# Experts: tokens sorted by expert group, so that a pair of experts works on two or three of four token tiles

## The chip, the cores and the metric

One core of one Trainium2 chip runs the whole program. The metric is device microseconds of one execution, as the median of the runs shown; lower is better. Engines are named as the profile names them: PE is TensorE's matmuls, PEld its weight loads, DVE VectorE, ACT ScalarE, POOL GpSimd, SP SyncE, which here only issues transfers.

## The reference

A decoder layer on 512 tokens of 1024 numbers, in float32: a mixer of four branches, cross attention into 256 memory tokens, and a mixture of experts. After each of the three, `x = layer_norm(alpha * x + y)`. The change touches the third part and the last layer norm:

```python
def hier_moe(x, rg_w, rg_b, re_w, re_b, w_gu, w_down):       # 512 tokens, 4 groups of 8 experts
    p_grp = softmax(xt @ rg_w + rg_b)                        # 4 groups
    grp = argmax(p_grp)                                      # one group for each token
    p_e = softmax((xt @ re_w + re_b)[rows, grp])             # 8 experts of that group
    top_p, top_i = top_k(p_e, 2)                             # two of them
    w = p_grp[rows, grp] * top_p / sum(top_p)
    expert_idx = grp * 8 + top_i
    # for each token: sum over its two experts of
    #   w * ((silu(x @ gate) * (x @ up)) @ down)             gate, up: 1024 x 512 each, down: 512 x 1024
```

## The kernel before

The tokens lie in four tiles of 128 rows, `xt[0]` to `xt[3]`, 1024 numbers each. After the cross attention, `spread(q)` (line 1196) normalises a tile in place and splits it into a high and a low part, `XH[q]` and `XL[q]`, since a float32 value goes through TensorE's one-pass form as two such parts. Routing follows tile by tile: `route` finds group and experts, `place` counts the rank of each token within its expert, and `sid` becomes 64 x expert + rank: every expert has 64 slots (`SLOT`), and no expert has more tokens than that in these inputs. `overflow` (line 1732), inside a runtime `If`, would serve the rest.

The expert stage, `moe` (line 1787), takes the 32 experts in 16 pairs p = 0 to 15, 128 slots a pair, and two pairs share one gather. For each pair, in this order on TensorE:
- `hidden`, eight steps k: the slots' inputs `xg` times gate and up weights, float32, two experts in the two halves of the array; each step uses two chunks of 512 KB. Then silu and product on ACT and DVE (`activate`), and four transposes (`turn`);
- `combine` of the pair before: for each token tile and half row two one-pass products with the one-hot matrix `ohT` (which slot feeds which token) add the weighted outputs `yh` and `yl` to `xt`, eight such groups;
- after odd pairs `gather` (with `collect` and `deliver`): for four column blocks and four token tiles, products of `XH` and `XL` with the one-hot matrices `oh` collect the tokens of the next 256 slots; ACT scales them by the second layer norm's gains and writes `xg`;
- `down`, four quarters of two chunks each, then `scaled` writes `yh` and `yl`.

In the first two pairs there is more: `route_weights` and `token_rows` (line 1389: the slot numbers and weights laid along rows, needed by `slot_rows`), `rejoin` (POOL adds `XH` and `XL` back into `xt`), `gains` and `regain` (the second layer norm's gain and bias on `xt`). The last two pairs run through `finish` (line 1599), written out by hand: `down` quarters, `spill` (their share of combine), `add`, `square`, and the third layer norm with the output, by halves of tiles; two halves (`SHARED`) are done on ACT and POOL.

Order: TensorE, VectorE and ScalarE keep the order of the code from line 1034 on, and SyncE's queue likewise in `moe`. The weights come through that queue, 24 chunks a pair, 384 in all, into a ring of 29 places (`chunk`, `eat`): a chunk is requested when the one 29 before it has been used up (`eat`). Seven further chunks of the first pair have places of their own (`once`), four of them in `xt`. So 36 chunks are there before the stage begins.

## Time and profile before

| | us |
|---|---|
| median of three runs | 1118.59 (1116.53 to 1119.81) |
| the profiled execution | 1120.17 |
| its span | 1118.5 |

| share of the span | PE | PEld | DVE | ACT | POOL |
|---|---|---|---|---|---|
| busy | 96% | 66% | 51% | 37% | 12% |

The page divides the span into 40 slices and shows busy shares in tenths; TensorE is at 9 in almost all, the DMA at 9 from slice 26 to 38, where it moves 408 to 409 GB/s. All times within the span are counted from its start. The expert stage begins near 618 us. A matmul in float32 is two records of the profile; records of the two halves of the array overlap, and matmul ends are modelled, so a busy PE is not PE at its peak.

### The profile page before, as it was taken

The numbers are of one execution on the slowest core, as the hardware profiler recorded it, in microseconds if no ns is written. First come the engines' busy times: TensorE is split into PE (matmuls) and PEld (weight loads), VectorE is DVE, ScalarE is ACT, GpSimd is POOL, SyncE is SP. The second block draws the span as 40 slices with busy tenths as digits, with TensorE's granted clock in tenths as the row PEclk, the third lists the DMA queues.
The fourth block names the chain that finished last, engine by engine and source line by source line (L and its number), as shares of the span: only waits on it lengthen the run. The fifth ranks groups of instructions, "written<-read, shape, count | busy, mean of one in ns | idle before, by whom it ended". The sixth has DMA issues, their size and how long they took to land. (4 is left out here: it accounts for less than half of the span.)

```text
span 1118.5 us, 15296 instructions
## 1 busy us (share of the span) xinstructions
PE 1073.0 (96%) x5818; PEld 741.9 (66%) x5818; DVE 571.4 (51%) x1214; ACT 408.5 (37%) x767; POOL 131.6 (12%) x131
## 2 busy tenths in 40 slices
PE   7999999999999999998998999999989999999993
PEld 6688777777888777787867555564655464656452
DVE  6436656878855633654558163524260433334426
ACT  6326647567544423433445312121203021212023
POOL 1000002302211112334124030000000000000003
PEclk9999999999999999998999899999999999999997
DMA  6612222112222213765363778999999999999982
GB/s 241 235 57 76 76 76 95 57 57 95 96 84 76 76 58 101 299 216 174 130 261 110 305 296 342 409 409 408 409 408 408 409 408 409 409 409 409 409 350 75
DMA packets 75052, 263.49 MB, mean 236 GB/s; under 512 B 8416, under 2 KB 8704, under 8 KB 74976
## 3 DMA queue, kind: packets, MB, share of 16 engines
q1 hardware_dynamic: 73440, 257.81, 60.2%
q0 software_dynamic: 1248, 4.15, 1.1%
q8 instruction: 47, 0.77, 0.3%
q10 hardware_dynamic: 288, 0.52, 0.1%
q14 instruction: 29, 0.24, 0.1%
HBM read 260.36 MB, written 2.10 MB: 235 GB/s over the span
## 5 line engine op out<-in xcount | busy, mean ns | idle before, releaser
L236 PE MATMUL acc<-ring,xg 128*64 128x512 f32 x724 | 167.6, 592 | 0.0
L228 DVE TENSOR_TENSOR wl<-raw,wh 128x1024 fp32r<-128x1024 f32 x63 | 78.5, 1247 | 88.9 <-PE mm L236 41.6
L236 PEld LDWEIGHTS acc<-ring,xg 128*64 128x64 f32 x724 | 54.3, 137 | 98.3 <-issue 94.0
L236 PE MATMUL mm<-XH,wh 128*128 128x512 f32 x392 | 106.1, 400 | 5.9 <-ACT XH L220 5.2
L227 ACT ACTIVATE wh<-raw 128x1024 fp32r<-128x1024 f32 x71 | 75.0, 1057 | 97.0 <-PE mm L236 59.0
L236 PE MATMUL mm<-XL,wh 128*128 128x512 f32 x392 | 106.7, 398 | 0.0
L236 PE MATMUL mm<-XH,wl 128*128 128x512 f32 x392 | 106.2, 397 | 0.0
L236 PEld LDWEIGHTS mm<-XH,wh 128*128 128x128 f32 x392 | 73.2, 190 | 23.7 <-ACT XH L220 5.2
L1596 DVE SCALAR_TENSOR_TENSOR yl<-t,ws,yh 128x512 fp32r<-128x512 f32 x28 | 20.8, 750 | 127.7 <-ACT yh L1595 127.7
L236 PEld LDWEIGHTS mm<-XH,wl 128*128 128x128 f32 x392 | 73.4, 189 | 18.8 <-issue 3.8
L236 PEld LDWEIGHTS mm<-XL,wh 128*128 128x128 f32 x392 | 73.0, 189 | 16.0 <-issue 1.2
L236 PE MATMUL t<-ring,hh 128*64 128x256 f32 x696 | 81.8, 381 | 0.0
L1557 ACT ACTIVATE hh<-acc 128x512 f32<-128x512 f32 x15 | 9.0, 597 | 173.2 <-PE acc L236 162.7
L1558 DVE TENSOR_TENSOR hh<-hh,acc 128x512 f32<-128x512 f32 x15 | 10.3, 688 | 117.7 <-PE acc L236 106.5
L236 PEld LDWEIGHTS t<-ring,hh 128*64 128x64 f32 x696 | 51.0, 137 | 27.0 <-issue 2.1
L1465 ACT ACTIVATE xg<-acc,gbt 128x128 f32<-128x128 f32 x128 | 47.9, 461 | 44.0 <-PE acc L236 44.0
L852 POOL TENSOR_TENSOR mix<-mix,gate 128x512 f32<-128x512 f32 x24 | 37.7, 1573 | 191.2 <-DVE gate L851 173.5
L1710 POOL TENSOR_TENSOR stat<-stat,mhalf 128x2 f32<-128x2 f32 x2 | 2.3, 1154 | 447.9 <-DVE stat L1709 447.9
L1595 ACT ACTIVATE yh<-t,ws 128x512 fp32r<-128x512 f32 x28 | 19.0, 688 | 82.2 <-PE t L236 69.2
L236 PE MATMUL s<-in,in 128*128 128x256 f32 (+5 forms) x198 | 43.8, 342 | 0.7 <-ACT S L626 0.7
L1497 DVE SCALAR_TENSOR_TENSOR xt<-xt,s 128x512 f32<-128x512 f32 x60 | 38.4, 681 | 7.9 <-PE s L236 7.9
L555 ACT ACTIVATE S<-S,sm 128x128 f32<-128x128 f32 (+3 forms) x48 | 26.6, 555 | 38.4 <-DVE sm L553 38.1
(449 smaller groups left out, 2011.1 us busy)
## 6 DMA issues: line engine op xcount, KB each, us to landing
ring<-gu SPq DMA_DIRECT2D x193, 512.0 KB, 10.2
ring<-dn SPq DMA_DIRECT2D x93, 512.0 KB, 10.2
XL<-gu SPq DMA_DIRECT2D x36, 512.0 KB, 10.2
raw<-wing SPq DMA_DIRECT2D x32, 512.0 KB, 3.3
raw<-gu SPq DMA_DIRECT2D x26, 512.0 KB, 10.2
XL<-dn SPq DMA_DIRECT2D x16, 512.0 KB, 10.2
raw<-winf SPq DMA_DIRECT2D x15, 512.0 KB, 3.2
raw<-dn SPq DMA_DIRECT2D x13, 512.0 KB, 10.2
```

What stands on the lines that cost most here:

```text
L227: self.nc.scalar.activation(h, r, AF.Copy)
L228: (self.nc.gpsimd if pool else self.nc.vector).tensor_tensor(l, r, f32(h), op=ALU.subtract)
L236: self.nc.tensor.matmul(out, lhsT, rhs, start=start, stop=stop, skip_group_check=True)
L555: nc.scalar.activation(s[:, :n], s[:, :n], AF.Exp, bias=sm[:, 0, q:q + 1], scale=-1.0, accum_out=sm[:, 1, q:q + 1])
L852: nc.gpsimd.tensor_tensor(mix[d], mix[d], g, op=ALU.add)
L1465: self.nc.scalar.activation(t[:, d, :], p[:, d - 2 * b, w * k:w * k + w], AF.Identity, scale=self.gbt[:, d:d + 1], bias=self.gbt[:, NK + d ...
L1497: self.nc.vector.scalar_tensor_tensor(z, z, scale, p, op0=ALU.mult, op1=ALU.add)
L1557: self.nc.scalar.activation(h, pg[0], AF.Silu)
L1558: self.nc.vector.tensor_tensor(h, h, pg[1], op=ALU.mult)
L1595: nc.scalar.activation(yh[:, cs], py[ch], AF.Copy, scale=ws)
L1596: nc.vector.scalar_tensor_tensor(yl[:, cs], py[ch], ws, f32(yh[:, cs]), op0=ALU.mult, op1=ALU.subtract)
L1710: nc.gpsimd.tensor_tensor(w(11), w(5), self.mhalf.to_broadcast([128, 2]), op=ALU.pow)
```

## The change

- In the routing stage, `records` puts what belongs to a token (experts, ranks, weights, its number, its group) into one tile `rec`; `sort` works out each token's place in an order sorted by group, and the routing weights are worked out there as well. `spread` also writes each normalised tile to memory (`zd`), by ACT's queue.
- In pair 0, `sort_records` moves the records into sorted order by products with the permutation, and `use_records` makes the index lists and marks tokens that lie outside the tiles that their group may use (`SPAN`); any such token sends the program into the overflow loop. `token_rows` now comes after `down`.
- `rejoin` fetches the rows of `zd` into `xt` by index, a transfer by POOL for each tile, instead of adding `XH` and `XL`. `respread` splits the sorted tiles again: tiles 0 and 1 in pair 1, ahead of its activation, tiles 2 and 3 in pair 2 with POOL.
- `gains` uses two other banks and gains scaled by alpha; `regain` runs on tiles 0 and 1 in pair 1 and on tiles 2 and 3 at the end of pair 2. Pair 1's order is now gains, turn, regain, gather, gains, regain, combine, down.
- `onehots`, `gather`, `slot_rows`, `combine` and `spill` run over the tiles of the group's span: two for the first and last four pairs, three for the others.
- Token tiles 0 and 1 are normalised and written out in pairs 9 and 13 (`settle`), tiles 2 and 3 at the end. All output goes through POOL by index (`ship`), at the end in halves of tiles. The gains of the third layer norm are loaded in pair 8 by POOL.

```diff
-SHARED = ((0, 0), (0, 1))
+SPAN = (0, 1), (0, 1, 2), (1, 2, 3), (2, 3)
...
     def gains(self, ps, ch):
...
-            p = self.t(ps, [128, 512], F32, "acc", 4)
+            p = self.t(ps, [128, 512], F32, "s", 2)
...
     def rejoin(self):
         self.xt = [self.t(self.right, [128, 1024], F32, f"xt{q}", 1) for q in range(NT)]
-        for cs in (slice(0, 512), slice(512, 1024)):
-            for q in range(NT):
-                self.nc.gpsimd.tensor_tensor(self.xt[q][:, cs], f32(self.XH[q][:, cs]), f32(self.XL[q][:, cs]), op=ALU.add)
-
-    def regain(self, ch, gb):
         for q in range(NT):
+            self.nc.gpsimd.indirect_dma_start(out=self.xt[q], out_offset=None, in_=self.zd[:, :],
+                                              in_offset=bass.IndirectOffsetOnAxis(ap=self.idx[:, q:q + 1], axis=0))
+
+    def respread(self, qs, low):
+        for q in qs:
+            self.nc.scalar.activation(self.XH[q], self.xt[q], AF.Copy)
+            low.tensor_tensor(self.XL[q], self.xt[q], f32(self.XH[q]), op=ALU.subtract)
...
             def spread(q):
                 z = self.xt[q]
                 nc.scalar.activation(z, z, AF.Identity, scale=stat[q][:, 5:6], bias=stat[q][:, 6:7])
+                nc.scalar.dma_start(self.zd[128 * q:128 * q + 128, :], z)
                 nc.scalar.activation(self.XH[q], z, AF.Copy)
...
             self.collect(hot[3], 3, range(4))
+            self.sort(mq, ps)
...
+    def sort(self, mp, ps):
...
+        p = self.t(ps, [128, 512], F32, "s", 2)
+        self.mm(p[:, 0:E], ones, self.cum[NT - 1], True, True)
+        self.mm(p[:, 64:80], ones, flat(run), True, False)
+        self.mm(p[:, 64:80], self.tri[:, 0:128], flat(grp), False, True)
+        nc.vector.tensor_tensor(flat(pr), p[:, 64:80], flat(grp), op=ALU.mult)
+        nc.vector.tensor_reduce(pos[:, 0], pr.rearrange("p g q -> p q g"), axis=AX.X, op=ALU.add)
+        nc.vector.tensor_scalar(pos[:, 1], pos[:, 0], -256.0, None, op0=ALU.add)
+        self.route_weights(mp, p)
+        self.pos = pos
+
+    def permutation(self, mp):
...
+            for i in range(2):
+                self.nc.vector.tensor_scalar(t[:, 256 * i:256 * i + 256], self.mc[:, _M_IOTA:_M_IOTA + 256], self.pos[:, i, q:q + 1], None, op0=ALU.is_equal)
+            self.perm.append(t)
+
+    def sort_records(self, ps):
+        p = self.t(ps, [128, 512], F32, "s", 2)
+        for t in range(NT):
+            for q in range(NT):
+                self.mm(p[:, 8 * t:8 * t + 8], self.perm[q][:, 128 * t:128 * t + 128], self.rec[:, q], q == 0, q == NT - 1)
+        return p
...
     def slot_rows(self, mp, p):
         nc = self.nc
+        span = SPAN[p // 4]
+        cs = slice(128 * span[0], 128 * span[-1] + 128)
...
     def gather(self, ps, oh, dst, work=iter(())):
         for b in range(4):
             p = self.t(ps, [128, 2, 256], F32, "acc", 4)
-            for q in range(NT):
-                self.collect(oh[q], q, [b], {b: p})
+            for q in oh:
+                self.collect(oh[q], q, [b], {b: p}, min(oh), max(oh))
...
-    def combine(self, ps, rows, ohT, yh, yl, scale=1.0, wide=False):
-        for i in range(2 * NT):
-            ch, q = divmod(i, NT)
+    def combine(self, ps, rows, ohT, yh, yl, tiles=range(NT), wide=False, sums={}):
+        for i in range(2 * len(tiles)):
+            ch, q = i // len(tiles), tiles[i % len(tiles)]
...
+    def ship(self, q, h=None):
+        if h is None:
+            ix, o, z = self.idx[:, q:q + 1], self.a["out"], self.xt[q]
+        else:
+            ix, o, z = self.idx2[:, q, h:h + 1], self.a["out"].rearrange("t (h c) -> (t h) c", h=2), self.xt[q][:, 512 * h:512 * h + 512]
+        self.nc.gpsimd.indirect_dma_start(out=o, out_offset=bass.IndirectOffsetOnAxis(ap=ix, axis=0), in_=z, in_offset=None)
+
+    def settle(self, q, stat):
+        for ch in range(2):
+            self.norm_square(stat, q, ch, self.t(self.m0, [128, 512], F32, "wt", 2))
+        self.norm_stats(stat)
+        self.norm_rstd(stat)
+        self.norm_apply(self.xt[q], stat, self.gb3)
+        self.ship(q)
...
         def spill(b, j):
-            for q in range(NT):
-                if j == 0 and q % 2 == 0:
+            for n, q in enumerate(span):
+                if j == 0 and n == 0:
...
         def apply(q, h):
-            z, _, b, o = part(q, h)
-            nc.vector.scalar_tensor_tensor(z, z, c(11, q), b, op0=ALU.mult, op1=ALU.add)
-            nc.sync.dma_start(o, z)
...
+            nc.vector.scalar_tensor_tensor(z, z, c(11, q), gb[1][:, cs], op0=ALU.mult, op1=ALU.add)
+            self.ship(q, h)
...
         centre(*halves[0])
         tt(5, 5, 10, ALU.add)
...
+        tt(5, 5, 8, ALU.add)
+        nc.gpsimd.tensor_tensor(v(11), v(5), self.mhalf.to_broadcast([128, 2]), op=ALU.pow)
+        for t in halves[1:]:
+            centre(*t)
+        for t in halves:
             apply(*t)
...
+            if p == 1:
+                self.respread((0, 1), nc.vector)
             h, hT = self.activate(mp, pg)
-            if p < 2:
-                gb = self.gains(ps, p)
+            if p == 0:
+                rec = self.sort_records(ps)
+            elif p == 1:
+                gb = self.gains(ps, 0)
             else:
                 for _ in range(4):
                     next(work, None)
             self.turn(ps, h, hT)
-            if p == 1:
-                self.regain(1, gb)
-                next(work)
-                next(work)
-                py = self.down(ps, hT, p)
-            elif p == 0:
-                self.route_weights(m1, ps)
-                self.token_rows(m1, ps)
+            if p == 0:
+                self.use_records(m1, rec, ps)
+            elif p == 1:
+                self.regain(0, gb, (0, 1))
             else:
                 for _ in work:
                     pass
             if p % 2 and p + 1 < n:
-                xgs = fetch(oh, work)
-            for _ in work:
-                pass
+                xgs = fetch(oh, iter(()))
+            if p == 1:
+                gb = self.gains(ps, 1)
+                self.regain(1, gb, (0, 1))
+                for _ in work:
+                    pass
+            if p == 2:
+                self.respread((2, 3), nc.gpsimd)
...
-            if p != 1:
-                py = self.down(ps, hT, p)
+            py = self.down(ps, hT, p)
             if p == 0:
+                self.token_rows(m1, ps)
                 ohT, ws = self.slot_rows(m1, p)
+                self.rejoin()
             done = (ohT, *self.scaled(py, ws))
-            if p == 0:
-                self.rejoin()
-                self.regain(0, gb)
+            if p == 2:
+                for ch in range(2):
+                    self.regain(ch, self.gains(ps, ch), (2, 3))
+            if p == 8:
+                self.gb3 = [self.t(self.wp, [128, 1024], F32, tag, 2) for tag in ("wh", "wl")]
+                src = self.a["ln3"]
+                for i in range(2):
+                    nc.gpsimd.dma_start(self.gb3[i], bass.AP(tensor=src.tensor, offset=src.offset + 1024 * i, ap=[[0, 128], [1, 1024]]))
+            if p in (9, 13):
+                self.settle(p // 12, stats[p // 12])
```

## Rows read from the trace of the kernel before

**Rows 1.** Windows, 40 us of the steady stage: window, its us, then columns as named.

```profile
core 0: us, PE busy (x) PEld busy (x) DVE busy (x) ACT busy (x) POOL busy (x), PEclk, DMA share, GB/s
880.00:920.00 40.00, 40.00 (x262) 25.39 (x262) 17.74 (x36) 9.20 (x21) 0.00 (x0) 1.00 1.03 409
```

**Rows 2.** The chain that ended last, pieces of pairs 9 and 10: start, us, what.

```profile
891.15 13.73 PE acc L236 x64
904.88 1.13 PE s L236 x4
...
908.31 8.60 PE acc L236 x68
916.91 7.06 PE t L236 x64
```

**Rows 3.** Windows, 4 us at the end of the stage.

```profile
1084.00:1088.00 4.00, 4.00 (x31) 2.89 (x29) 0.48 (x1) 2.63 (x10) 0.00 (x0) 1.00 0.61 243
```

**Rows 4.** Timeline of PE, last down product: start, us, what.

```profile
1098.17 1.08 PE L236 MATMUL s<-ring,oh 128*64 128x256 f32 x8
```

**Rows 5.** Windows, 2 us around the start of the expert stage.

```profile
616.00:618.00 2.00, 2.00 (x12) 2.00 (x11) 0.00 (x0) 1.90 (x6) 0.00 (x0) 0.50 0.39 158
620.00:622.00 2.00, 2.00 (x12) 0.69 (x10) 0.00 (x0) 1.98 (x7) 0.00 (x0) 1.00 0.13 29
```

**Rows 6.** Windows, 2 us in the first two pairs.

```profile
642.00:644.00 2.00, 2.00 (x15) 1.28 (x16) 0.92 (x3) 0.60 (x1) 0.00 (x0) 0.75 0.04 14
650.00:652.00 2.00, 2.00 (x12) 0.56 (x9) 1.63 (x3) 0.92 (x2) 2.00 (x2) 1.00 0.00 0
684.00:686.00 2.00, 2.00 (x13) 0.96 (x13) 0.00 (x0) 1.43 (x5) 0.00 (x0) 1.00 0.23 92
```

**Rows 7.** Waits of SP's queue, 640 to 660 and 680 to 700: us, times, longest.

```profile
SPq L1512 <- PE t L236: 11.1, 1, 11.1
...
SPq L1512 <- PE acc L236: 13.5, 7, 9.2
```

**Rows 8.** Timeline of ACT, PE and DVE in pair 0.

```profile
616.10 5.70 ACT L1465 ACTIVATE xg<-acc,gbt 128x128 f32<-128x128 f32 x16 [5.85 <-PE acc L236]
618.55 3.92 PE L236 MATMUL t<-ring,xg 128*64 128x512 f32 x16
635.25 0.19 DVE L1378 TENSOR_REDUCE wsc<-s 128x1 f32<-128x32 f32 x1 [1.14 <-PE s L236]
637.25 0.19 ACT L1383 ACTIVATE wsc<-wsc 128x4 f32<-128x4 f32 x1
```

**Rows 9.** Timeline of PE, small float32 products.

```profile
590.79 1.88 PE L236 MATMUL s<-rw,zT 128*128 128x40 f32 x16
632.69 2.05 PE L236 MATMUL acc<-ident,gbt 128*128 128x128 f32 x16
```

**Rows 10.** Timeline of PE, first products of pair 1, then its down products.

```profile
649.43 1.88 PE L236 MATMUL acc<-raw,xg 128*64 128x512 f32 x8
666.78 7.13 PE L236 MATMUL t<-ring,hh 128*64 128x256 f32 x64
```

**Rows 11.** Tile xt, regain: duration min/median/max in ns, starts, forms.

```profile
L933 DVE TENSOR_TENSOR xt<-xt,acc x8: 677/680/689, 651.7 to 669.2; 128x512 f32<-128x512 f32 x8
```

**Rows 12.** Timeline of DVE in the tail.

```profile
1105.25 0.75 DVE L1704 SCALAR_TENSOR_TENSOR xt<-xt,stat,xg 128x512 f32<-128x512 f32 x1
...
1107.90 1.75 DVE L1704 SCALAR_TENSOR_TENSOR xt<-xt,stat,xg 128x512 f32<-128x512 f32 x1
```

**Rows 13.** DMA issues: count, KB each, median us to landing.

```profile
out<-xt SPq DMA_DIRECT2D x6, 256.0 KB, 2.1
...
S<-cst POOLq DMA_DIRECT2D x1, 256.0 KB, 2.9
...
rw<-rw POOLq DMA_DIRECT2D x1, 160.0 KB, 16.2
```

**Rows 14.** Timeline of POOL, issue of four plain loads.

```profile
452.70 2.18 POOL L941 DMA_DIRECT2D xt<-x  x4 [4.12 <-PE acc L236]
```

More of the change, by code (lines that the diff above doesn't have):

```diff
@@ L1432, in onehots @@
             out += [self.last(g) for g in steps[i:i + 2]]
-        return out
+        return dict(zip(tiles, out))
     def last(self, g):
@@ L1528, in load_first @@
         first = self.in_ring[:self.ring_size]
-        for j in first + [22, 18, 19, 23, 20, 21, 15]:
+        for j in first + [22, 23, 15, 18, 19, 20, 21]:
             if j in self.once:
```

158 lines of the change are left out of this document (98 added, 60 removed).

## The prediction, made before the result was known

> **What bounds the kernel now.** I read the windows first, then the chain of work, then the fine windows around the start of the expert stage, then its end. In the steady part of that stage two resources are full at once: TensorE is busy 40.00 of 40 us at full clock, and the DMA moves 409 GB/s [rows 1]. The chain of what ended last runs through TensorE alone. Its pieces give a pair's price: 13.73 us of hidden products, 7.06 of down products, combine in four pieces of 0.93 to 1.13, two of its eight groups in each, and in every second pair 7.66 more for the gather (the 8.60 piece holds a combine piece of 0.94) [rows 2]. With 0.44 for the transposes, two pairs take 2 x (13.73 + 7.06 + 3.93 + 0.44) + 7.66 = 58.0 us. Their weights are 48 chunks of 512 KB. At 409 GB/s one chunk takes 1.28 us, so 61.5 us. TensorE is therefore slightly faster than the data and lives on the 36 chunks that were loaded before the stage began. At the end it has not used up that lead: in 1084 to 1088 the queue still moves 0.97 MB [rows 3], which is what the two ln3 tensors behind the last weights need, so the last weight lands at about 1084.0. TensorE finishes with it at 1098.17 + 1.08 = 1099.25 [rows 4].
>
> So the stage has two floors close together, and taking TensorE work away can win only the lead that is left, unless the data also comes sooner. The refills flow from 622 (620 to 622 still moves 29 GB/s [rows 5]). 384 - 36 = 348 chunks take 446.1 us, which would end at 1068. The missing 15.9 us are stretches in which the queue had no free slot: 14 GB/s at 642 to 644, 0 at 650 to 652, 92 at 684 to 686 [rows 6], with waits for TensorE of 11.1 us and 13.5 us on the queue [rows 7]. Slots come free when TensorE has eaten a chunk, so the first two pairs decide this.
>
> **What the change takes away.** The inputs, run through the reference, put 105, 154, 163 and 90 tokens in the four groups. Sorted, the groups end at rows 105, 259, 422 and 512, inside the spans that the change allows, so the overflow loop stays empty. For pairs 1 to 13 combine falls from 8 groups to 4 or 6 (3.93/8 = 0.49 us each): 3 x 4 + 8 x 2 + 2 x 4 = 36 groups, 17.6 us. The gathers for pairs 4 to 15 lose a quarter of 7.66 four times and half of it twice, 15.3 us. The eight spills at the end lose half of their eight products of 0.12 (7.66/64), 3.8. That is 36.7 us of TensorE work. By itself, and with about 7 us for the two gain passes that move into pair 2, TensorE would end near 1069. The data can't: the bound moves to the DMA from the middle of the stage on.
>
> **What it does to the data, step by step.**
> Before the first pair, ACT gets two Exp (the routing weights) ahead of the 16 deliveries that fill the first expert's input. They need three products queued behind the last gather of the routing stage (about 619), then three small DVE operations and the chain that took 635.25 to 637.44 before, table load of 1.28 included [rows 8]. The deliveries, which began at 616.10 under that gather, begin at about 620.5 (621.7 with a load), the first hidden product at 621.0 instead of 618.55 [rows 8]. I take +2.4 us (2.2 to 3.5).
> Hidden products of pair 0 end at 635.1. The 16 record products are 32 records at 1.88/16 [rows 9], 3.8 us; the transposes 0.5; a product waits 1.5 for six small DVE operations; down starts at 640.4 (before 642.0) and ends at 647.8. The token rows, formerly ahead of it, now follow, at two of the prices of 2.05 for 16 records [rows 9]: 651.9, where pair 1 starts (before 649.43 [rows 10]).
> Refills: 15 slots from 624.4 take to 643.6; the next two are freed at about 642.2, so the first gap (some 4 us) closes. The queue then has nothing until pair 1's first products are eaten, about 655.2. In that hole the gather of 2 MB by index (5.1 us at 409) is free, and the gap left is 3.7 us (before 4.6).
> Pair 1 ends its hidden products at 665.6. Then come gains 2.05, transposes 0.5, the gather of half size 3.8, gains again 2.05, its regains (0.68 an operation [rows 11]) and four combine groups through two banks, 3.6. Down starts at 677.6; before it started at 666.78 [rows 10]. Pair 1's hidden slots keep the queue busy to 675.7, the next come at 681.0: a gap of 5.3, where before about 4 us were lost at 684 and 1 at 690.
> From there 307 chunks remain, at 691.3 instead of effectively 688.6: +2.7 us. In the full stretch the change adds the ln3 tensors (1 MB, formerly behind the last weight) and the scatter of two finished token tiles (1 MB): 5.1 us. The last weight lands at 1084.0 + 2.7 + 5.1 = 1091.8.
> After it come half a down quarter, a spill and the other half, 0.9 + 0.6 + 0.9 = 2.4: 1094.2 instead of 1099.25. **-5.0 us.**
> At no cost: the permutation's one-hots and the record arithmetic (DVE is idle in 620 to 622 [rows 5]), the four writes of rows to memory (158 GB/s at 616 to 618), the splitting again of tiles (ACT, DVE, then POOL, under hidden products), and the two early layer norms, on engines that are under half busy [rows 1]. If a wait on TensorE lost such cover, it would cost nothing as long as the ring is waiting for data anyway.
>
> **The tail** after the last down product is 1118.5 - 1099.25 = 19.25 us. Before, DVE did twelve half-tile operations; seven step by 0.66, but five by 1.67, beside POOL's products on the shared halves (those at 1105.25 and 1107.90 in [rows 12]). The change has eight at 0.66 and no POOL product, so -7.0, and fewer sums and squares, -0.7. The output leaves through POOL: 2.9 us to landing for 256 KB against 2.1 on SP [rows 13], +0.8. How long POOL is busy issuing a transfer by index is in no row; the lower bound is the plain 0.55 [rows 14], and I take twice that, 1.1, since 128 rows are addressed one by one. Four issues from the first apply end 2.4 after the last apply. Sum -7.7 + 0.8 + 2.4 = **-4.5 us** (bounds: -6.3 at 0.55; +2.2 if each scatter waits until the one before has landed, about 3.5 a piece).
> The Trainium skill, page "SBUF — State Buffer", section "Who interferes with whom", says that a DVE instruction with two SBUF inputs and a GpSimd instruction that reads SBUF exclude each other. The 1.67 agrees. It also says that POOL can't write descriptors while DVE holds the shared port; by that the four issues would follow the last apply, and the tail would be 2.0 us longer. No row here shows it.
>
> **Rivals.**
> 1. *Chained scatters.* All four last scatters name the whole output; if each waits for its forerunner, the tail ends 6.7 us later: 1116, no change that can be told. For it: nothing in the program tells which rows an index list writes.
> 2. *Slow clock.* A TensorE that waits for each chunk has 1.72 us of work in every 2.56. The clock fell to 0.50 at 616 to 618, behind the waits of the routing stage, and was 1.00 at 620 to 622 in unbroken work [rows 5]. If it is low when the last chunks land, the 2.4 us double and a few quarters run late: +2.4 to +5, 1112 to 1114. The Trainium skill, page "TensorE: Matmul & The Clock Gate", section "HAM oscillation — how this bites in real kernels", speaks against the change here: waits for data between short bursts put the clock back each time. In this kernel a slow clock makes TensorE the bound and so busy again, which is why I price only the end.
> 3. *A late gather: slower.* Splitting tiles 0 and 1 stands ahead of pair 1's activation on ACT and DVE. Their rows are asked for at about 645 and needed by 662. Beyond that each microsecond delays pair 1's down products, their slots and the end. POOL's loads landed between 2.9 and 16.2 us after issue [rows 13], inside the cover. If the rows of one transfer went through one of 16 DMA engines (25.6 GB/s, 20.5 us a tile), tile 1 would land at 686: +24, 1133 and more with the scatters. It becomes slower from about 30 us.
> 4. *Better:* the two gaps left (9.0 us) vanish because TensorE gets through pairs 0 and 1 as fast as before: 1100.
> 5. *The change doesn't do what it says:* tokens outside their span would start the overflow loop, eight rounds over all weights, some 3.9 ms. The counts above exclude it nearly.
>
> **How the numbers follow.** Against the profiled execution's own 1120.17 us (span 1118.5), -9.5 gives 1110.7; that execution stands 1.6 above the median 1118.59, so the forecast is 1109. A measurement of this kernel can tell about 0.3% from no change, so faster means under 1115.2, slower over 1121.9. Chances: the forecast with its bounds (1104 to 1115) 0.46, slow clock 0.10, better 0.06, chained scatters 0.20, late gather 0.12, the early gaps twice as long 0.05, overflow 0.01. Faster 0.62, same 0.20, slower 0.18. The range reaches from the better case to the edge of slower, 1101 to 1124.
>
> **What would show it.** Right: the DMA at 409 GB/s from about 691 to the last weight at about 1092, TensorE idle in the second half of the stage between chunks, some 25 us in all, the DMA's gap near 642 gone, pair 1's down products 10 us later, the last down product near 1094, applies at 0.66. Wrong: TensorE still busy without a break to the end; the last weight before 1086 or after 1096; the activation of pair 1 waiting for a copy of gathered rows; scatters one landing apart.

## The result, and the profile after

The changed kernel takes 1127.99 us (median of 4 runs, 1127.36 to 1129.02). The kernel before took 1117.56 us beside it (1116.16 to 1119.81). The ratio is 1.0092, with a 95% interval of 1.0072 to 1.0113: 0.9% slower. The forecast was 1109, and its range began at 1101 and ended at 1124, so the sign and the range were both wrong.

The profiled execution took 1128.08 us with a span of 1126.4, 7.9 more than the 1118.5 of before. Its windows first (window, its us, busy time and count by engine, then the clock, the DMA's share and GB/s); they answer [rows 1], [rows 3] and [rows 6].

```profile
core 0: us, PE busy (x) PEld busy (x) DVE busy (x) ACT busy (x) POOL busy (x), PEclk, DMA share, GB/s
638.00:640.00 2.00, 1.48 (x8) 0.94 (x9) 1.70 (x14) 0.60 (x1) 0.00 (x0) 0.51 1.04 414
640.00:642.00 2.00, 2.00 (x12) 1.14 (x10) 0.35 (x3) 0.00 (x0) 0.00 (x0) 0.50 1.02 406
642.00:644.00 2.00, 2.00 (x13) 1.03 (x12) 0.00 (x0) 0.00 (x0) 0.00 (x0) 0.50 0.66 256
...
678.00:682.00 4.00, 4.00 (x28) 2.37 (x30) 2.05 (x3) 0.00 (x0) 0.00 (x0) 1.00 0.06 20
...
880.00:920.00 40.00, 39.49 (x266) 22.37 (x264) 12.78 (x32) 11.17 (x26) 0.24 (x1) 1.00 1.03 409
...
1040.00:1080.00 40.00, 32.31 (x148) 10.70 (x144) 10.07 (x26) 3.01 (x8) 2.23 (x3) 1.00 1.03 410
...
1088.00:1092.00 4.00, 4.00 (x29) 2.68 (x28) 0.30 (x2) 0.71 (x2) 0.00 (x0) 1.00 0.94 377
1092.00:1096.00 4.00, 4.00 (x30) 2.49 (x27) 1.60 (x7) 1.58 (x6) 0.00 (x0) 1.00 0.41 168
1096.00:1100.00 4.00, 4.00 (x23) 2.48 (x23) 0.48 (x1) 1.08 (x5) 0.00 (x0) 1.00 0.01 4
```

Three things are to be seen. In 1040 to 1080 TensorE is busy for 32.31 of 40 us while the DMA is full: the data bounds the stage from its middle on, as forecast. At the end this turns round: from 1088 to 1100 TensorE has no gap, and the DMA runs dry. What it still moves from 1088 on, (377 + 168 + 4) x 4 us, is 5.4 us at 409 GB/s, which would be through near 1093.4; the prediction took its 1084.0, and from it 1091.8, from the bytes of a window in a like way. It thins out instead: the last chunk was requested at 1086.2 and landed some 10.1 us later, near 1096.3 (in the kernel before 1076.6 and 10.2, near 1086.8). And at 678 to 682 the queue stands still, while at 638 to 644 the clock is 0.50.

The last ten down chunks (first and last request, then the time to landing):

```profile
L1598 SPq DMA_DIRECT2D ring<-dn x10: 327/327/328, 1074.7 to 1086.2; - x10
DMA to landing us min/median/max: 10.0/10.1/10.2
```

Now TensorE's timeline (start, us, engine, line, operation, count, idle time before it and what ended it), which answers [rows 4], [rows 8] and [rows 10].

```profile
618.72 0.17 PE L239 MATMUL s<-grp,tri 128*128 128x16 bf16 x1
620.43 1.94 PE L239 MATMUL t<-ring,xg 128*64 128x512 f32 x8 [1.54 <-ACT xg L1550]
...
653.16 1.94 PE L239 MATMUL acc<-raw,xg 128*64 128x512 f32 x8
...
679.39 7.13 PE L239 MATMUL t<-ring,hh 128*64 128x256 f32 x64
...
1078.57 1.94 PE L239 MATMUL acc<-XL,xg 128*64 128x512 f32 x8 [0.63 <-DMA XL<-gu]
1080.43 0.74 PE L239 MATMUL acc<-yh,ohT 128*128 128x256 f32 x4
1081.37 0.66 PE L1651 MATMUL t<-ident,hh 128*128 128x128 f32 x4 [0.19 <-DVE hh L1644]
1082.50 0.43 PE L239 MATMUL s<-XL,oh 128*64 128x256 f32 x1 [0.47 <-ACT oh L1654]
1082.51 0.43 PE L239 MATMUL s<-raw,oh 128*64 128x256 f32 x1
...
1086.77 1.94 PE L239 MATMUL s<-ring,oh 128*64 128x256 f32 x8
...
1093.57 1.95 PE L239 MATMUL t<-ring,hh 128*64 128x256 f32 x16
...
1102.22 1.08 PE L239 MATMUL s<-ring,oh 128*64 128x256 f32 x8
```

The first line is the last product of the routing stage, the second the first hidden product, 1.88 later than before. The line at 1078.57 is the last hidden group of pair 15, and it waited for its chunk. From there to 1103.30 nothing waits for data any more: from 1082.50 on, the first of the down products, quarters of 1.95 and spills of 0.74 follow each other (the products of a quarter's two experts start 0.01 apart and run side by side). Their records overlap by 0.07 to 0.08, so a quarter moves the work on by 1.87 and a spill by 0.66.

The tail, DVE and POOL, and the landing of the transfers by index (count, median us to landing); this answers [rows 12] and [rows 13].

```profile
1109.60 2.73 DVE L1803 SCALAR_TENSOR_TENSOR xt<-xt,stat,wl 128x512 f32<-128x512 f32 x4
```

```profile
1110.63 1.28 POOL L1690 DMA_INDIRECT out<-xt,idx  x1 [1.69 <-DVE xt L1803]
1114.42 0.98 POOL L1690 DMA_INDIRECT out<-xt,idx  x1 [2.51 <-issue]
1118.28 0.97 POOL L1690 DMA_INDIRECT out<-xt,idx  x1 [2.87 <-issue]
1121.75 0.97 POOL L1690 DMA_INDIRECT out<-xt,idx  x1 [2.50 <-issue]
```

```profile
out<-xt,idx POOLq DMA_INDIRECT x6, 2.9
xt<-zd,idx POOLq DMA_INDIRECT x4, 5.6
```

The four applies are done at 1112.33, some 0.66 apart. The scatters start 3.5 to 3.9 apart, which is one issue and one landing (0.97 + 2.9 = 3.87).

In the sections below the span is cut into four lengths: the start of the first hidden product; from there to the end of the last hidden product (H); from there to the end of the last down product (D); from there to the end of the span (tail). Executions differ by some us in when the expert stage begins (614.33 to 621.38 in three kernels that are the same up to there; the profiled execution of e1, at 1115.28 us, is an early one), so the lengths are compared rather than the times. In the four kernels that equal the changed one up to the last hidden product, H is 459.7 to 460.4; in two that equal the kernel before, it is 455.1 and 453.0. The expectations of e5 and e6 count to the start of the last hidden group (458.1 in the changed kernel), and that of e11 puts the border between H and D some 0.9 earlier (456.5 and 20.1); the sums are the same. The ratios are each against the kernel before, timed beside them: 1117.12 us for e1 to e4, 1116.80 for e5 to e8, 1116.32 for e9 to e11, 1116.52 for e12.

| kernel | first hidden | H | D | tail | median us | ratio to before, 95% |
|---|---|---|---|---|---|---|
| before | 618.55 | 455.06 | 25.64 | 19.25 | 1117.56 | |
| after | 620.43 | 460.08 | 22.79 | 23.10 | 1127.99 | 1.0072 to 1.0113 |
| e1_unchain | 614.33 | 460.35 | 22.79 | 16.13 | 1121.11 | 1.0001 to 1.0048 |
| e2_plain_tail | 621.38 | 459.72 | 22.81 | 12.69 | 1117.45 | 0.9990 to 1.0022 |
| e3_finish | 619.90 | 465.01 | 17.35 | 23.14 | 1125.95 | 1.0053 to 1.0117 |
| e4_cut_alone | 617.99 | 450.20 | 22.79 | 19.72 | 1111.62 | 0.9919 to 0.9961 |
| e5_down_first | 620.32 | 458.39 | 22.77 | 23.12 | 1126.06 | 1.0056 to 1.0106 |
| e6_exp_late_ln3_early | 618.40 | 459.39 | 22.79 | 23.12 | 1125.75 | 1.0055 to 1.0106 |
| e7_whole_quarters | 619.73 | 459.88 | 19.18 | 23.11 | 1123.66 | 1.0037 to 1.0082 |
| e8_all_four | 618.84 | 457.34 | 19.21 | 16.11 | 1113.10 | 0.9942 to 0.9979 |
| e9_before_whole | 618.07 | 453.04 | 22.00 | 19.29 | 1113.85 | 0.9960 to 0.9990 |
| e10_no_gather | 617.02 | 460.33 | 22.81 | 22.64 | 1126.97 | 1.0065 to 1.0119 |
| e11_all_and_late | 618.81 | 454.20 | 19.18 | 16.11 | 1110.39 | 0.9934 to 0.9974 |
| e12_no_ln3_load | 619.57 | 451.47 | 19.20 | 16.46 | 1107.90 | 0.9891 to 0.9950 |

After against before: +1.88 at the start, +5.02 in H, -2.85 in D, +3.85 in the tail, together +7.90.

### The profile page after: what moved, and what is told of

The parts are those of the page before. It is cut to its first block, busy times and chain, and to the rows that moved or that the text cites. A ratio compares the mean times of both kernels' runs of the same rounds, so it can differ in the third digit from the quotient of the medians.

```text
span 1126.4 us, 14844 instructions
## 1 busy us (share of the span) xinstructions
PE 1049.7 (93%) x5613; PEld 708.8 (63%) x5613; DVE 536.0 (48%) x1188; ACT 405.5 (36%) x759; POOL 130.6 (12%) x136
## 5 line engine op out<-in xcount | busy, mean ns | idle before, releaser
L239 PE MATMUL acc<-ring,xg 128*64 128x512 f32 x724 | 172.7, 597 | 17.2 <-DMA ring<-gu 17.2
L1550 ACT ACTIVATE xg<-acc,gbt 128x128 f32<-128x128 f32 x128 | 45.6, 478 | 7.0 <-PE acc L239 7.0
L239 PE MATMUL acc<-XL,xg 128*64 128x512 f32 x132 | 38.6, 595 | 1.3 <-DMA XL<-gu 1.2
L239 PE MATMUL acc<-raw,xg 128*64 128x512 f32 x104 | 34.1, 642 | 4.7 <-DMA raw<-gu 2.9
## 6 DMA issues: line engine op xcount, KB each, us to landing
ring<-gu SPq DMA_DIRECT2D x193, 512.0 KB, 10.2
ring<-dn SPq DMA_DIRECT2D x93, 512.0 KB, 10.2
XL<-gu SPq DMA_DIRECT2D x36, 512.0 KB, 10.2
raw<-gu SPq DMA_DIRECT2D x26, 512.0 KB, 10.2
XL<-dn SPq DMA_DIRECT2D x16, 512.0 KB, 10.2
raw<-dn SPq DMA_DIRECT2D x13, 512.0 KB, 10.2
```

The lines of the kernel that those rows point to most:

```text
L239: self.nc.tensor.matmul(out, lhsT, rhs, start=start, stop=stop, skip_group_check=True)
L1550: self.nc.scalar.activation(t[:, d, :], p[:, d - 2 * b, w * k:w * k + w], AF.Identity, scale=self.gbt[:, d:d + 1], bias=self.gbt[:, NK + d ...
```

## The experiments

### The chain of scatters: e1_unchain and e2_plain_tail

In e1 each scatter gets a view of the output of its own, so that nothing in the program makes one wait for another; in e2 the last four are plain transfers from SP.

```
-            ix, o, z = self.idx2[:, q, h:h + 1], self.a["out"].rearrange("t (h c) -> (t h) c", h=2), self.xt[q][:, 512 * h:512 * h + 512]
+            ix, o, z = self.idx2[:, q, h:h + 1], self.views[2 * q - 2 + h].rearrange("t (h c) -> (t h) c", h=2), self.xt[q][:, 512 * h:512 * h + 512]
...
-        self.ci = 0
+        self.ci, self.views = 0, dram_disjoint_views(self.a["out"], 6)
```

```
-            self.ship(q, h)
+            nc.sync.dma_start(self.a["out"][128 * q:128 * q + 128, cs], z)
```

> The changed kernel, with the output given to the program as six views that it may take as disjoint, one for each scatter; every engine's instructions and their order stay the same, only the waits of the scatters go. Theory (the last four scatters wait for each other's landing): in the changed kernel they start at 1110.63, 1114.42, 1118.28 and 1121.75, 3.5 to 3.9 apart; without the waits each follows its apply, or the scatter before it by POOL's 1.0 to 1.3 of issue, so the last starts near 1114.3 instead of 1121.75 and the span shrinks by 7 to 7.5, to about 1119 (1120.7 us). Rival A (POOL needs that long to write the addresses of 128 rows, or can't write them beside DVE): the starts stay about 3.5 apart, and nothing is gained. Rival B (the writes themselves are slow in memory): issues move together, but each lands later by what it starts sooner; gain under 2.

> The changed kernel, but the four last half tiles go out by a plain transfer from SP, to the rows in sorted order: the output rows of two token tiles stand in another place, all other work is the same. Theory (chain): the last apply ends at 1112.33, a plain transfer lands 2.1 later, and the program ends about 1.7 after that: a span near 1116, 10 less than the 1126.4 of the changed kernel (1118 us); what it gains over the run without the chain, about 3, is the price of leaving through POOL by index. Rival (the applies, not the scatters, hold the end): no more than 2 less than the changed kernel.

DVE and POOL in the tail of e1:

```profile
1103.77 2.73 DVE L1803 SCALAR_TENSOR_TENSOR xt<-xt,stat,wl 128x512 f32<-128x512 f32 x4
```

```profile
1104.79 1.28 POOL L1690 DMA_INDIRECT out<-xt,idx  x1 [1.68 <-DVE xt L1803]
1106.38 0.98 POOL L1690 DMA_INDIRECT out<-xt,idx  x1 [0.30 <-issue]
1107.67 0.97 POOL L1690 DMA_INDIRECT out<-xt,idx  x1 [0.30 <-issue]
1108.94 0.97 POOL L1690 DMA_INDIRECT out<-xt,idx  x1 [0.30 <-issue]
```

The same four instructions now start 1.3 to 1.6 apart, and the tail is 16.13 instead of 23.10: the waits cost 7.0. Rivals A and B both fall. By plain transfers the tail is 12.69, so leaving through POOL by index costs 3.4 more than four plain stores. Here the Trainium skill, page "SBUF — State Buffer", section "Who interferes with whom", can be weighed: it says that descriptors that GpSimd has to write starve while DVE holds the shared port. It also says of `tensor_tensor`, as inferred, that with two SBUF inputs it takes only the read side of that port, while writing descriptors needs the write side. The applies too have two such inputs, so the prediction's "by that the four issues would follow the last apply" does not follow from the section. In e1 the first scatter was issued at 1104.79, between the applies that ran from 1103.77 to 1106.50, and took 1.28 instead of 0.97. So these rows show a delay of at most 0.3 us, not the 2.0 that the prediction gave as its price.

### The finish: e3_finish, e7_whole_quarters and e9_before_whole

e3 moves two down quarters of pair 14, with their chunks, ahead of the last hidden chunks:

```
-        order = [*range(n - 32), *range(n - 24, n - 16), *quarter(0, 0), *range(n - 16, n - 8)]
+        order = [*range(n - 32), *range(n - 24, n - 16), *quarter(0, 0), *range(n - 16, n - 12), *quarter(0, 1), *range(n - 12, n - 10), *quarter(0, 2), *range(n - 10, n - 8)]
...
+        hidden(4)
+        hidden(5)
+        spill(0, 0)
+        down(1, 0, 0, 1)
+        scale(1, 0)
+        hidden(6)
+        down(2, 0, 0, 1)
+        scale(2, 0)
+        hidden(7)
+        last.append(turn(lambda: spill(1, 0)))
...
```

e7, and e9 on the kernel before, compute two quarters with both experts side by side:

```
-        down(1, 1, 0)
+        down(1, 1, 0, 1)
         spill(1, 0)
-        down(1, 1, 1)
...
-        down(2, 1, 0)
+        down(2, 1, 0, 1)
         spill(3, 0)
-        down(2, 1, 1)
```

> The changed kernel, with the second and third down quarter of pair 14 (products and chunks alike) moved ahead of the last hidden chunks of pair 15, so that 10 chunks instead of 14 follow the last hidden one. No work is added or taken away. Theory (the finish is bound by TensorE: from the last hidden chunk on it had 20.8 us of unbroken work for 17.9 us of data, after an activation gap of 2): the last weight still lands at about 1093.7, TensorE uses its idle time before that, and the last down product ends 2.4 to 4 after the landing instead of 9.6, at 1096 to 1098: 5.5 to 7 us less, 1121 to 1122.5. Rival A (the finish waits for data, as the prediction had it: last landing + 2.4): no change. Rival B (the moved scaling and combining hold PSUM banks that the activation needs): slower by 1 to 3.

> The changed kernel, with the two down quarters of the finish that were computed one expert at a time (b=1 and b=2 of pair 15) computed with both experts side by side, as all others are: the same 16 products each, in 1.95 instead of about 1.9 for each expert's eight. Theory (from the last hidden chunk to the end TensorE never waits, so work there counts in full): the 23.65 us from the start of the last hidden products to the start of the last eight down products fall by 3 to 3.7. Rival (the prediction's view, that this stretch ends a fixed 2.4 behind the last chunk): no change, or later by up to 1 since a quarter then waits for both its chunks.

> The kernel before, with the two split down quarters of the finish computed with both experts side by side; nothing of the change. Theory (TensorE is unbroken to the end there, so its work counts in full): the same 3.6 us as in the changed kernel, 1113 to 1114, with the last weight landing where it did. So what the run with all four repairs gains over the kernel before would be no merit of the sorting. Rival (there a quarter would wait for its second chunk): under 1.

TensorE in e3, the last two hidden groups:

```profile
1077.85 1.94 PE L239 MATMUL acc<-XL,xg 128*64 128x512 f32 x8 [0.62 <-DMA XL<-gu]
...
1082.97 1.94 PE L239 MATMUL acc<-raw,xg 128*64 128x512 f32 x8 [0.62 <-DMA raw<-gu]
```

e3 won 0.5 us in the stage (H + D 482.36 instead of 482.87) and 2.0 in the median, far from the 5.5 to 7 expected; its ratio can't be told from the changed kernel's. D fell by 5.4, as the work moved; but H rose by 4.9. A quarter moved ahead of the last hidden chunk delays that chunk by 2 x 1.28 = 2.56, and takes 1.87 + 0.66 = 2.53 off the work behind it. The expectation had forgotten the first half of this. It gives no verdict against a finish bound by TensorE; a test has to change the amount of work. e7 does that.

TensorE in e7:

```profile
1085.87 1.95 PE L239 MATMUL s<-ring,oh 128*64 128x256 f32 x16
...
1097.71 1.08 PE L239 MATMUL s<-ring,oh 128*64 128x256 f32 x8
```

The 16 products take 1.95 side by side; in the changed kernel eight of them alone took 1.94 (at 1086.77). D falls from 22.79 to 19.18, by 3.61, the whole of the work saved. So from the last hidden chunk on it is TensorE that sets the end. In the kernel before, the same edit takes D from 25.64 to 22.00, by 3.64, and the time by 0.25% (ratio 0.9975; 2.5 us of medians, less than the 3.6 expected). So it is a gain that has nothing to do with the sorting.

### The cut by itself: e4_cut_alone

The main lines of its edit:

```
-            return self.onehots(self.sid, 256)
+            return self.onehots(self.sid, 256, SPAN[qd // 2] if qd > 1 else range(NT))
...
-            work = iter(()) if done is None else self.combine(ps, 128, *done, scale=ALPHA if p == 1 else 1.0, wide=p > 1)
+            work = iter(()) if done is None else self.combine(ps, 128, *done, scale=ALPHA if p == 1 else 1.0, wide=p > 1, tiles=SPAN[(p - 1) // 4] if p > 1 else range(NT))
...
-            for q in range(NT):
-                if j == 0 and q % 2 == 0:
+            for q in (2, 3):
+                if j == 0 and q == 2:
```

> The kernel before, with the cut of TensorE's work alone: combine for pairs 1 to 13 over 2 or 3 of 4 token tiles, gathers for pairs 4 to 15 over the same spans, the last spills over two tiles, 36.7 us of products in all. Tokens are not sorted, so rows outside the spans are left out of the sums; nothing is moved through memory, the start of the stage and the tail are those of before. Theory (data bounds the stage from the middle on, and the finish hangs on the last hidden chunk): the last weight lands at 1084 as before, TensorE stands idle between chunks in the second half by some 25 us in all, and the last down product ends about 9.6 after the landing, at 1093.7, instead of 1099.25: 5.5 us less, 1112 to 1113. Rival A (TensorE bounds the whole stage): the cut is worth its 36.7 less what is hidden, 1085 to 1095. Rival B (a TensorE that waits between chunks loses its clock, or the refills come later): no gain, 1117 or more.

TensorE at the end of e4 and a window of its second half:

```profile
1066.25 1.94 PE L236 MATMUL acc<-XL,xg 128*64 128x512 f32 x8 [0.62 <-DMA XL<-gu]
...
1089.90 1.08 PE L236 MATMUL s<-ring,oh 128*64 128x256 f32 x8
```

```profile
1000.00:1040.00 40.00, 34.41 (x198) 16.02 (x196) 7.22 (x14) 8.25 (x20) 0.00 (x0) 1.00 1.03 409
```

TensorE waits for data here too, and the end comes where D puts it: the last hidden group waits for its chunk, and D is 22.79 to the hundredth, as in the changed kernel. The cut of 36.7 us of work is worth 0.6%, 5.5 us of medians (1111.62 against 1117.12), as expected; rivals A and B fall. The lengths of the two profiled executions give more, 4.9 in H and 2.85 in D, less 0.5 in the tail, so 7.2. But 2.0 of this is not the cut: in the profiled execution of the kernel before, the clock fell to 0.50 at 640 to 642, and in e9, which is the same kernel up to its finish, the clock stayed at 1.00 there and H is 453.04, as against 450.20 in e4. The mechanism of the forecast, a cut that the data swallows, holds.

### Where the changed kernel's data is late: e5, e6, e10, e11 and e12

H is 9.9 us longer in the changed kernel than with the cut alone. The windows of the first 92 us after the first hidden product, in this order, of the kernel before, of e9 (the same kernel in this stretch), the changed one, e4 and e10:

```profile
618.55:710.55 92.00, 90.19 (x564) 50.91 (x565) 39.19 (x80) 21.96 (x45) 9.91 (x8) 0.98 0.85 330
```

```profile
618.07:710.07 92.00, 90.19 (x572) 50.55 (x573) 40.92 (x83) 23.15 (x48) 9.92 (x8) 1.00 0.88 342
```

```profile
620.43:712.43 92.00, 89.24 (x557) 49.08 (x557) 32.21 (x82) 24.77 (x50) 8.62 (x6) 0.96 0.89 341
```

```profile
617.99:709.99 92.00, 89.51 (x569) 49.44 (x570) 39.64 (x82) 23.11 (x48) 9.89 (x8) 1.00 0.88 340
```

```profile
617.02:709.02 92.00, 89.23 (x557) 48.87 (x557) 34.81 (x82) 24.74 (x50) 14.99 (x10) 0.96 0.82 317
```

92 us by the last column are 31.37 MB for the changed kernel. Less the gather of 2.10 MB, 29.27 MB are weights; in e4 all 31.28 are, and in e9 all 31.46. The 2.01 MB that are missing take 4.9 us at 409 GB/s. The other 2.1 MB (ln3, two early tiles) move in the full stretch: 5.1. Together 10.0, for the 9.9 measured. The kernel before itself had 30.36 MB in its profiled execution, with the clock at 0.98 in the mean of this stretch, where e9 and e4 have 1.00. In the changed kernel the clock fell as well (0.96); in e7 it was low for about half as long (0.98), and H is only 0.2 shorter (459.88), so the clock explains little of its late weights. The five runs take this apart.

In e5 the down products of pair 1 stand ahead of the gather. In e6 two moves were meant: the exponentials behind the deliveries, and the ln3 loads at pair 0. In e10 the tiles are rebuilt in SBUF in place of the gather from memory. The three edits, in this order:

```
-                self.regain(0, gb, (0, 1))
+                self.regain(0, gb, (0, 1)); py = self.down(ps, hT, p)
```

```
-        self.route_weights(mp, p)
...
-        self.permutation(m1)
+        self.permutation(m1); self.route_weights(m1, None)
...
-            if p == 8:
+            if p == 0:
```

```
-            self.nc.gpsimd.indirect_dma_start(out=self.xt[q], out_offset=None, in_=self.zd[:, :],
-                                              in_offset=bass.IndirectOffsetOnAxis(ap=self.idx[:, q:q + 1], axis=0))
+            for cs in (slice(0, 512), slice(512, 1024)):
+                self.nc.gpsimd.tensor_tensor(self.xt[q][:, cs], f32(self.XH[q][:, cs]), f32(self.XL[q][:, cs]), op=ALU.add)
```

> The changed kernel, with the down products of pair 1 straight behind its transposes, ahead of the gather, the gain passes and the first combine; nothing else moves. Theory (in the early part the queue stands still for want of eaten chunks: 41, 0 and 205 GB/s in the three stretches from 678 to 684): pair 1's down products start at about 671 instead of 680, the hole closes, and as data bounds everything behind it, the way from the first to the last hidden product, 458.1 us in the changed kernel, falls by 4 to 5. Rival A (the hole only moves, to where the late gather leaves TensorE without chunks to eat): under 2. Rival B (TensorE, not data, sets the way): 0. The rest of the program as in the changed kernel.

> The changed kernel with two moves that show at different places. One: the two exponentials of the routing weights stand behind the 16 deliveries on ACT, not ahead of them. Theory: the first hidden product comes 1.5 to 2.4 earlier against the end of the routing stage's last gather product (in the changed kernel the first delivery starts right behind the second exponential); rival: the deliveries wait for that gather anyway, 0. Two: the two ln3 tensors (1 MB) are loaded at pair 0, beside the hole of the refills, instead of at pair 8 in the full stretch. Theory (every MB in the full stretch is paid): the way from the first to the last hidden product falls by 1.3 to 2.6 from 458.1; rival (a short transfer fits beside the others, or what it takes early is lost there): 0.

> The changed kernel, with the four token tiles of the sum rebuilt on POOL from what is in SBUF, as the kernel before did, in place of the gather of 2 MB by index from memory: rows and sorted tokens then don't belong together, all other work is the same. The prediction had the gather free, in a hole of the refills: then the way from the first to the last hidden product stays at 460.1 us (end of the last hidden one). Rival (the hole is refilled late because the queue shares the engines with the gather, its weights at 16 us behind pair 0's end fewer by 2 MB): 2 to 5 less.

Windows of e5, to be read beside 678 to 682 of the changed kernel above:

```profile
678.00:682.00 4.00, 4.00 (x36) 4.00 (x36) 0.00 (x0) 2.96 (x9) 0.00 (x0) 1.00 1.03 407
...
686.00:690.00 4.00, 3.95 (x16) 1.44 (x17) 3.82 (x7) 1.27 (x2) 0.00 (x0) 1.00 0.70 281
690.00:694.00 4.00, 4.00 (x20) 1.30 (x18) 1.77 (x8) 0.00 (x0) 0.00 (x0) 1.00 0.78 259
```

The hole at 678 to 682 is closed (407 GB/s instead of 20), but 686 to 694 lose (128 + 150) x 4 us = 1.1 MB against 409 GB/s, since TensorE has gather, gain passes and combine to do from 677.9 to 687.9, where pair 2 begins, and eats no chunk meanwhile. H falls by 1.7: nearer to rival A (the hole moves) than to the 4 to 5 expected.

TensorE in e6, the last product of the routing stage and the first hidden one:

```profile
618.30 0.17 PE L239 MATMUL s<-grp,tri 128*128 128x16 bf16 x1
618.40 4.08 PE L239 MATMUL t<-ring,xg 128*64 128x512 f32 x18
```

0.10 lie between their starts, where the changed kernel has 620.43 - 618.72 = 1.71: the exponentials ahead of the deliveries cost 1.6, as expected. The second half of e6 tested nothing: the ln3 loads were issued at 827.4 as they were at 830.0 in the changed kernel, since the places in SBUF that they go to are in use until the overflow check at pair 7. Its 0.7 in H is hardly outside what equal kernels differ by.

e10: H is 460.33, as in the changed kernel, and the bytes of its window, 29.16 MB, are the changed kernel's weights within 0.1 MB. The gather from memory is free in the hole, as the prediction had it, and the rival falls. What is left for the 2.01 MB is that TensorE eats its first chunks late: pair 1's down products start 58.96 behind the first hidden product, in e4 46.36. This is found by exclusion; e5, which starts them at 50.41, gets back 1.7 of the 4.9.

e11 takes the scatters of the two early tiles to where the last weights land; e12, beside that, leaves out the ln3 load:

```
-        self.ship(q)
...
         add(1)
         tt(9, 0, 1, ALU.add)
+        late = self.t(mp, [128, 2], I32, "late"); nc.vector.tensor_copy(late, self.idx[:, 0:2])
+        for q in range(2):
+            nc.gpsimd.indirect_dma_start(out=self.views[q], out_offset=bass.IndirectOffsetOnAxis(ap=late[:, q:q + 1], axis=0), in_=self.xt[q], in_offset=None)
```

```
-        self.gb3 = [self.t(self.wp, [128, 1024], F32, tag, 2) for tag in ("wh", "wl")]
+        self.gb3 = [f32(self.XH[0]), f32(self.XL[0])]
```

> The run with all four repairs, with its 2 MB of other transfers out of the stretch in which the queue is full: the ln3 tensors are loaded between the routing stage and the first refill, where the queue moves 29 to 158 GB/s, and the two early token tiles are scattered when the last weights land (their index copied by DVE behind the second sum of the finish). Nothing of the computation is left out. Theory (every MB in the full stretch is paid at 409 GB/s): the way from the first to the last hidden product, 456.5 us, falls by 4 to 5, the finish goes back from 20.1 to 19.2, the tail stays 16.1: 1107 to 1109, 0.8 to 0.9% faster than the kernel before. Rival A (as with ln3 at pair 0, most of what is saved is lost elsewhere): 1112. Rival B (two late scatters on POOL hold the power that the last scale needs): 1 to 3 later in the tail.

> The run with all repairs and late scatters, without the load of the two ln3 tensors (1 MB): the last layer norm reads its scale and offset from the same two places in SBUF as before, which then still hold token tile 0, so the output's values are others; all other work is the same. The two runs that were to move this load earlier did not: it was issued at 827 to 830 in both, since the places it goes to are in use until the overflow check. Theory (a MB in the full stretch costs 1,048,576 bytes by 409 GB/s, 2.56 us, and moving the scatters out had gained 3.1 for the other MB): the way from the first to the last hidden product falls by 2.6, from 454.2 to 451.6, finish and tail stay at 19.2 and 16.1. Rival (what data gains there is lost to TensorE, which bounds that way by now): under 1.

POOL in e11:

```profile
1086.09 1.06 POOL L1769 DMA_INDIRECT out<-xt,late  x1 [49.45 <-DVE late L1767]
...
1096.67 1.16 POOL L1812 TENSOR_TENSOR stat<-stat,mhalf 128x2 f32<-128x2 f32 x1 [8.23 <-DVE stat L1738]
```

The scatters went out at 1086, and the power at 1096.67 waited for DVE, not for them. H falls from 457.34 (e8) to 454.20, by 3.1, though ln3 did not move (issued at 828.5); less than the 4 to 5 that both MB were to bring. e12 prices the other MB: H 451.47, 2.7 less, for 2.6 expected. So a MB in the full stretch costs 3.1 and 2.7, about its 2.56 us each time, as the theory of both runs has it; e11 fell short of its number because only one of the two MB was moved. With both gone, and pair 1 in e5's order, H is 1.3 above the cut alone.

### All repairs together: e8_all_four (and e11)

> The changed kernel with everything that the runs so far point to: scatters that don't wait for each other, pair 1's down products first, exponentials late and ln3 early, whole quarters in the finish. Nothing of the computation is left out. Theory (the four costs lie one behind the other on the path): 7.0 in the tail, 4 to 5 and 1.3 to 2.6 in the early part, 1.5 to 2.4 at the start, 3 to 3.7 in the finish: 17 to 21 less than the changed kernel's 1128, 1107 to 1111, so 0.6 to 0.9% faster than the kernel before. Rival (they cover each other, the early ones above all since refills then wait elsewhere): 1112 to 1117, no difference from the kernel before that can be told.

The four costs add up in part: 16.1 in the tail (7.0 less), 19.21 in D (3.6 less), 457.34 in H (2.7 less), 1.6 at the start. The median is 1113.10, 0.4% faster than the kernel before. That lies in the range of the rival (1112 to 1117), not in the theory's; but the rival's "no difference that can be told" is wrong too, since the interval (0.9942 to 0.9979) stays clear of 1. What is missing is ln3, which stayed where it was (2.7 by e12), and the hole of pair 1, which only moved. With the scatters late (e11) it is 1110.39, ratio 0.9954 (0.9934 to 0.9974): faster than the kernel before, and than the kernel before with whole quarters (1113.85), by 3.5 us of medians. That is what the sorting is worth once most of what came with it is repaired; the ln3 load is not.

## Why the prediction was wrong, step by step

The steps that held. Data bounds the stage from its middle on. The 360 us that follow those 92, before and after:

```profile
710.55:1070.55 360.00, 355.88 (x2162) 197.00 (x2160) 134.95 (x277) 66.16 (x144) 0.00 (x0) 1.00 1.03 409
```

```profile
712.43:1072.43 360.00, 332.88 (x1978) 167.98 (x1976) 113.71 (x260) 67.23 (x151) 5.64 (x8) 0.99 1.03 409
```

TensorE's busy time falls from 355.88 to 332.88, 23 us more idle time (forecast: some 25), and the clock was 1.00 in 1040 to 1080, so the rival of the slow clock fell. Here the Trainium skill, page "TensorE: Matmul & The Clock Gate", section "HAM oscillation — how this bites in real kernels", tells of a kernel whose short bursts of products alternate with longer waits for data and which loses the clock at each wait. Here the waits are 0.6 us between groups of 1.94, the clock stays, and no run shows the page's case.

The first hidden product was forecast for 621.0 and came at 620.43; that it is so near is luck, since executions differ by up to 7 there, and the exponentials cost 1.6 (e6), not 2.4. Pair 1 started at 653.16 (forecast 651.9): the stretch at 0.50 of the clock, 638 to 644, fell on pair 0's down products. Its down products started at 679.39 (677.6). The gather was free and not late, so that rival fell too; applies took 0.66.

The last weight, counted as the prediction did, was through at 1093.4 (1091.8), late by 1.6; by its landing it came 9.5 later than before (7.8 forecast). The +2.7 for late weights in the first two pairs came out against the trace that it was read from (30.36 less 29.27 MB, 2.7 us), but by luck: that execution had lost 1.1 MB against e9, with its clock low, and beside e4 the late weights cost 4.9. The sum of that step doesn't close either, since 307 chunks from 688.6 on end at 1082.1, not at 1084.0; only the difference of 2.7 went into the forecast.

First step that failed: "After it come half a down quarter, a spill and the other half, 0.9 + 0.6 + 0.9 = 2.4". The last down product ended at 1103.30, 9.9 behind the 1093.4 of the prediction's way of counting (7.0 behind the landing of the last weight), not 2.4. Of the 9.1 us between the forecast 1094.2 and this, 7.5 are this term, and 1.6 the later weight. The end hangs on the last *hidden* chunk: behind it lie 22.79 us of TensorE work (a spill and the transposes beside the activation, seven quarters of 1.87, of which two are split and cost it twice, and six more spills of 0.66), and this is more than the 14 chunks that still come behind it need at 1.28, 17.9. [rows 2] had the price of a quarter (7.06 / 4 = 1.77), and the line-up of chunks was in the code; the sum was simply not made. A look at the last chunk alone hides that TensorE is behind by then. e4 shows this term without any other part of the change, e7 that it is work and not waiting.

Second step that failed: the tail, forecast at 14.75 and measured at 23.10. 7.0 of the 8.35 are the chain of scatters (e1). This was rival 1, priced at 6.7 and given a chance of 0.20; its reason, that nothing in the program tells which rows an index list writes, was a fact of the program and should have made it the likeliest case. The rest, 1.4, is what e1's tail of 16.13 has above the forecast. In the kernel before, DVE's last operations were

```profile
1111.25 4.08 DVE L1704 SCALAR_TENSOR_TENSOR xt<-xt,stat,xg 128x512 f32<-128x512 f32 x3
```

and ended 16.08 behind the last down product; in e1 it is 9.03, so DVE gave 7.05 instead of 7.7. Behind DVE's end the span went on for 3.17 before and 7.10 in e1, 3.93 more instead of 3.2: four issues took from 1104.79 to 1109.91, 5.1 instead of 4.4, and ended 3.4 instead of 2.4 behind the last apply.

Put together: forecast -5.0 before the tail and -4.5 in it, measured +4.05 and +3.85. The 5.1 for 2 MB in the full stretch were about right as a price (3.1 and 2.7 in e11 and e12), and e11 avoids half of them; what the cut itself brought, 5.5 (e4), did not cover them, the 4.9 of late weights in the first pairs and the chain.

## What to carry to other kernels

When two resources take turns as the bound, cost the end from the last item that the late work depends on (here the last hidden chunk), adding all of the work behind it, and compare that with the data that is still to come; the landing of the last byte alone says little. A transfer by index names its whole tensor to whatever tracks dependencies, so here successive ones waited for each other until they were given views of their own: look at the spacing of their starts. What moved here in a stretch in which the queue was full cost about its time at the full rate, so put such a transfer before, after, or in a hole, and check in the trace that it did move. And hold a length from one execution against a second one of the same code before a gain is read from it: H of the kernel before was 455.06 once and 453.04 once.

## What the runs showed of the hardware that was not expected

- Eight products of one expert (64 columns of weights, 256 moving) took 1.94 us, and sixteen of two experts 1.95: a product of each starts 0.01 us behind the other's and they run side by side, so one expert alone wastes half of the time.
- POOL took 0.97 us to issue a scatter of 256 KB by index, with 0.30 between two; the first of a series took 1.28, and a gather of 512 KB 0.94 to 1.10. The scatters landed after 2.9 us (median of the six of the changed kernel; 2.8 for the four at the end of e11), against 2.1 for a plain store of the same size (the kernel before and e2).
- TensorE's clock was granted at 0.50 from 638 to 644, and the record products of 8 columns ran ahead of it. The kernel before, which has none, had 0.50 at 640 to 642, behind a wait of 1.81 for DVE; e9 and e4, with the same products and waits of 1.80 and 1.81, stayed at 1.00 there. So the same code came out either way, that wait alone does not make the clock fall each time, and what the small products do was not tried.
